# Short-convolution layer on one core: product e of the input projection also by seven smaller products in ten chunks, with 26 instead of 32 pages

## The chip, the core and the metric

The kernel runs on one core of a Trainium2 chip. The metric is the device time of one execution in microseconds. Before the change its median over 3 runs is 773.18 us (772.85 to 773.5). The engines are named as in the profile: PE is TensorE's matmul, PEld its weight load, DVE is VectorE, ACT is ScalarE, POOL is GpSimd, and SP is SyncE, which issues most of the DMAs.

## The reference

One layer (`DEPTH = 1`), so only the short-convolution mixer is computed. `x` is 1 x 1024 x 1024 in float32.

```python
u = rms_norm(x, pre_norm)
z, bg, cg, v = jnp.split(u @ w_in, 4, axis=-1)          # w_in: 1024 x 8192
y = bg * causal_dwconv(cg * v, conv_w) * jax.nn.silu(z)  # conv of width 3 along the sequence
m = y @ w_out                                            # w_out: 2048 x 1024
out = x + rms_norm(m, post_norm)
```

## The kernel before, in words

**The input projection.** The 2048 inner channels are cut into 16 chunks `c` of 128. Each chunk has two pairs of channel blocks, `p = 2c` for (`cg`, `v`) and `p = 2c + 1` for (`z`, `bg`). For one pair the product of a 2 x 2 block matrix of weights with the 2 x 2 block matrix of activations is computed by Winograd's form of Strassen's rule: seven products `a` to `g` in place of eight. Each is 128 channels by 512 positions with 512 rows to sum over, so four slices `k`. In float32 accuracy a product of one slice is three matmuls in the format fp32r: low part of the weights by high part of the activations, high by low, high by high. A product of one pair is therefore 12 matmuls with 512 columns. Names: `u_a` to `u_g` are the activations of a product; `wah`, `wal` to `wgh`, `wgl` the high and low parts of its weights; `raw` the loaded weight blocks; `se`, `sc`, `sf`, and `raw` overwritten for `d`, the sums of weight blocks that the rule asks for, made on POOL or DVE; `px`, `pv`, `py` the PSUM banks that collect the products; `sna`, `snc`, `sne` copies of a bank in SBUF to which later banks are added.

**Seven smaller products.** For `b`, `f` and `g` the rule is applied a second time in most chunks (`by_seven`): the 2 x 2 blocks are then the two pairs of a chunk by two halves of 256 rows, and the positions are halved too. Each of the seven sub-products `a'` to `g'`, for the two pairs together, is six matmuls with 256 columns. Their weight sums are `dsb`, `dsf`, `dsg`, their split weights `dwb`, `dwf`, `dwg`, their activations `ub..._deep` and so on, their PSUM banks `px2b`, `py2b`, `pv2b` and so on. Products `a`, `c`, `d` and `e` are done whole, pair by pair.

**Splitting.** A weight `t` is split by an ACT copy that rounds to fp32r (`wah`) and a DVE subtraction `t - wah`. In `split` that subtraction reads both operands from SBUF. In `split_by_bank` ACT also copies `t` into a PSUM bank, `beside`, and the subtraction reads one operand from there. Before the change there is one such bank, held for the whole of the projection and reused by every copy.

**After the projection.** The convolution is one ACT multiplication and two DVE steps over 1024 positions per chunk (`cv<-gpad,cw,cv`), in chunk `c + 1`'s time. The output projection (`po_`, `pb_`, `pf_` banks) is another pass by the same rule.

**What sets the order.** All instructions are first recorded; then `Plan.arrange` puts each engine's instructions in an order, by due times that go back from PE's order and by costs that the planner assumes, with a table `boost` that moves the due time of single instructions. PE's own order is written out by the list `slots`, a list of products and sub-products. Each engine then runs its list strictly in order, and waits at an instruction until its operands and its buffer are there. SBUF buffers of 2 KB per partition, the pages, hold all weights, sums and copies; there are `PAGES` of them, and a load on SP waits in its queue until its page is free. PSUM has eight banks in one pool. All instructions are issued in one helper, so nearly all have the line L252 in the profile before.

Of the kernel before, what the change touches and what calls it, by code (L numbers as in the profile page):

```python
# [18 lines left out]
PAGES = 32  # L19
DEEP = 2  # L20
DEEP_F = 2
DEEP_G = 2
LEAD = 7.0
HEAD_SLOTS = (
    0, 23, 31, 30, 29, 28, 27, 26, 25, 24, 22, 21, 20, 1, 19, 18, 2, 17, 16, 15, 14, 3, 13, 12, 11, 10, 4, 7, 9, 8,
    5, 6, 31, 29, 30, 28, 23, 0, 10, 11, 27, 26, 7, 4, 29, 15, 31, 16, 13, 3, 21, 22, 1, 20, 26, 27, 25, 30, 4, 7,
)
PLAN = {
    "end": 14.0,
    "psum": 3.0,  # L30
    "store": 6.0,
    "turns": 1,
    "apart": 11.0,
    "hard": 2.0,
    "lock": 0.3,
    "sum": 10.0,
# [578 lines left out]
def kernel(  # L615
# [70 lines left out]
    ug_d = dram.tile([P, KH, HB], F32, tag="ug_d", name="ug_d")  # L686
    uf_d = dram.tile([P, CQ // 2, HB // 2], F32, tag="uf_d", name="uf_d")
# [1378 lines left out]
```

## Time and profile before

| what | before |
|---|---|
| median of 3 runs | 773.18 us |
| profiled execution | 772.83 us |
| its span | 771.0 us, granted clock 0.998 |
| PE busy | 762.2 us (99%), 4320 matmuls |
| DVE busy | 673.9 us (87%), 1022 instructions |
| ACT busy | 458.8 us (60%), 880 instructions |
| POOL busy | 462.2 us (60%), 416 instructions |
| DMA | 130.11 MB, mean 169 GB/s |

The profiled execution is 1.8 us longer than its span; what lies around the span is taken as unchanged. Busy time is the union of an engine's instructions. A matmul's duration in the trace is longer than the distance to the next matmul, since matmuls overlap in the array; what counts for the time is the distance from start to start.

### The profile page before, as it was taken

The numbers are of one execution on the slowest core, as the hardware profiler recorded it, in microseconds if no ns is written. First come the engines' busy times: TensorE is split into PE (matmuls) and PEld (weight loads), VectorE is DVE, ScalarE is ACT, GpSimd is POOL, SyncE is SP. The second block draws the span as 40 slices with busy tenths as digits, with TensorE's granted clock in tenths as the row PEclk, the third lists the DMA queues.
The fourth block names the chain that finished last, engine by engine and source line by source line (L and its number), as shares of the span: only waits on it lengthen the run. The fifth ranks groups of instructions, "written<-read, shape, count | busy, mean of one in ns | idle before, by whom it ended". The sixth has DMA issues, their size and how long they took to land.

```text
span 771.0 us, 12816 instructions
## 1 busy us (share of the span) xinstructions
PE 762.2 (99%) x4320; PEld 669.6 (87%) x4320; DVE 673.9 (87%) x1022; ACT 458.8 (60%) x880; POOL 462.2 (60%) x416
## 2 busy tenths in 40 slices
PE   8999999999999999999999999999999999999996
PEld 7888889898889898888888898988888889889885
DVE  6899988989988978989999989798999898877993
ACT  7765678575656565556556565556653656564831
POOL 2519997889575778696789777584739100600321
PEclk9999999999999999999999999999999999999999
DMA  9222325243333547576858474927465998666842
GB/s 318 66 56 82 119 85 152 101 126 131 97 116 96 171 111 209 126 191 158 239 137 254 116 215 107 249 84 213 122 180 174 335 367 293 197 218 206 274 150 109
DMA packets 117137, 130.11 MB, mean 169 GB/s; under 512 B 7320, under 2 KB 74704, under 8 KB 116944
## 3 DMA queue, kind: packets, MB, share of 16 engines
q1 hardware_dynamic: 112560, 120.77, 49.0%
q0 software_dynamic: 4352, 8.39, 7.1%
q8 instruction: 34, 0.56, 0.3%
q14 instruction: 31, 0.25, 0.1%
q10 hardware_dynamic: 160, 0.14, 0.0%
HBM read 101.74 MB, written 44.30 MB: 189 GB/s over the span
## 4 chain that ended last, share of the span: by engine, by line
PE 98%; DVE 1%; DMA 0%; ACT 0%; POOL 0%; issue 0%; POOLq 0%; ACTq 0%
PE px L252 39%; PE pv L252 15%; PE po_x L252 11%; PE px2b L252 5%; PE px2f L252 4%; PE px2g L252 3%; PE po_v L252 3%; PE pp L252 3%; PE pv2b L252 3%; PE pv2f L252 2%; PE pf_x L252 1%; PE pb_x L252 1%; PE py2b L252 1%; PE pv2g L252 1%; PE py L252 1%; PE pf_v L252 1%
## 5 line engine op out<-in xcount | busy, mean ns | idle before, releaser
L252 PE MATMUL px<-u_d,wdh 128*128 128x512 f32 x248 | 76.8, 390 | 0.0
L252 PE MATMUL px<-u_a,wah 128*128 128x512 f32 x248 | 76.7, 390 | 0.0
L252 PE MATMUL pv<-u_e,weh 128*128 128x512 f32 x248 | 76.7, 390 | 0.0
L252 PE MATMUL px<-u_c,wch 128*128 128x512 f32 x248 | 76.6, 390 | 0.0
L252 ACT COPY beside<-raw 128x512 f32<-128x512 f32 x67 | 39.6, 591 | 31.8 <-DVE wal L252 11.0
L252 PEld LDWEIGHTS px<-u_d,wdh 128*128 128x128 f32 x248 | 46.6, 188 | 9.1
L252 PEld LDWEIGHTS px<-u_c,wch 128*128 128x128 f32 x248 | 46.7, 188 | 9.0
L252 PEld LDWEIGHTS px<-u_a,wah 128*128 128x128 f32 x248 | 46.7, 188 | 8.9
L252 PEld LDWEIGHTS pv<-u_e,weh 128*128 128x128 f32 x248 | 46.6, 188 | 8.9
L252 DVE SCALAR_TENSOR_TENSOR cv<-gpad,cw,cv 128x1024 f32<-128x1024 f32 x32 | 49.7, 1554 | 3.4 <-ACT cv L252 3.3
L252 POOL TENSOR_TENSOR sf<-raw,sc 128x512 f32<-128x512 f32 x30 | 44.5, 1482 | 10.9 <-DVE sc L252 6.0
L252 PE MATMUL px<-u_d,wdl 128*128 128x512 f32 x124 | 48.7, 393 | 0.0
L252 PE MATMUL px<-u_a,wal 128*128 128x512 f32 x124 | 48.7, 393 | 0.0
L252 PE MATMUL px<-u_c,wcl 128*128 128x512 f32 x124 | 48.5, 392 | 0.0
L252 PE MATMUL pv<-u_e,wel 128*128 128x512 f32 x124 | 48.5, 391 | 0.0
L252 POOL TENSOR_TENSOR sc<-se,raw 128x512 f32<-128x512 f32 x25 | 36.5, 1460 | 19.0 <-DVE se L252 10.0
L252 ACT COPY sna<-px 128x512 f32<-128x512 f32 x30 | 17.6, 586 | 49.4 <-PE px L252 47.7
L252 POOL TENSOR_TENSOR raw<-raw,raw 128x512 f32<-128x512 f32 x31 | 44.8, 1446 | 3.3 <-DVE se L252 1.9
L252 POOL TENSOR_TENSOR rs_post<-ve_post,minus_half 128x1 f32<-128x1 f32 x7 | 5.4, 784 | 68.1 <-DVE ve_post L252 68.1
L252 POOL TENSOR_TENSOR se<-raw,raw 128x512 f32<-128x512 f32 x22 | 33.1, 1504 | 17.7 <-DMA raw<-in_sc_w_in 5.7
L252 DVE TENSOR_TENSOR wcl<-sc,wch 128x512 fp32r<-128x512 f32 x31 | 31.6, 1020 | 2.6 <-ACT wch L252 2.6
L252 DVE TENSOR_TENSOR sna<-px2b,sna 128x256 f32<-128x256 f32 x56 | 23.2, 413 | 11.9 <-PE px2b L252 11.9
(486 smaller groups left out, 2637.1 us busy)
## 6 DMA issues: line engine op xcount, KB each, us to landing
raw<-in_sc_w_in SPq DMA_DIRECT2D x128, 256.0 KB, 4.6
y_d<-cv SPq DMA_DIRECT2D x16, 512.0 KB, 3.1
s_d<-s SPq DMA_DIRECT2D x32, 256.0 KB, 4.8
t_d<-in_sc_w_out POOLq DMA_DIRECT2D x16, 512.0 KB, 8.2
tb<-in_sc_w_out SPq DMA_DIRECT2D x16, 256.0 KB, 3.0
t_d<-in_sc_w_out SPq DMA_DIRECT2D x16, 256.0 KB, 4.5
t_d<-t_d SPq DMA_DIRECT2D x16, 256.0 KB, 4.5
s<-y_d SPq DMA_DIRECT2D x16, 256.0 KB, 4.7
```

Source lines behind the costliest of these rows:

```text
L252: getattr(engine, name)(*(self.plain(a) for a in args), **{k: self.plain(a) for k, a in kw.items()})
```

## The change

1. `by_seven` takes in `e`: in chunks 4 to 13, ten of them, product `e` of both pairs is computed by seven sub-products of 256 columns. Their accumulators are `px2e`, `pv2e` and the two `pv` banks; `deep_after_e` puts them together through the pages `es0`, `es1`. Weight sums are `dse`, split weights `dwe`, activations `ue..._deep`, made once under chunk 3 from a copy of `u_e` kept in DRAM (`ue_d`).
2. In these chunks PE does `e` first: its sub-products stand under `c`, `d` and `a` of the chunk's first pair, those of `b` begin only behind them, and all of `f` and `g` follow in the second pair. The copy `sne` of the first pair now starts from `d`'s bank, and `e` is added later.
3. `PAGES` goes from 32 to 26, and the pool of split activations from 18 to 24 buffers. In the ten chunks the lower weight rows for `g` are loaded a second time (`fetch_far`, tiles `rg`), so that the first copy's pages are given back before; the early weight splits of the head move to a pool of their own.
4. `beside` takes any free PSUM bank for each copy and gives it back. Also `wc`, `dwf1`, `dwg0` to `dwg2` and the new `dwe0` to `dwe2` are split through a bank.
5. The planner's numbers and the `boost` table are new.

```diff
-PAGES = 32
+PAGES = 26
+DEEP_E = 4
...
-        0: -1.88, 1: 31.37, 2: -1.93, 4: 16.59, 5: 18.27, 6: 0.14, 20: 0.84, 21: 1.2, 22: 10.67, 27: -0.09,
+        7: -0.46, 56: -1.96, 59: 1.16, 101: 0.11, 164: -0.46, 165: -3.22, 184: -0.96, 201: -0.26, 206: -0.48,
...
-BY_BANK_DEEP = (("b", 0), ("b", 1), ("b", 2), ("f", 0), ("f", 2))
+BY_BANK_DEEP = (("f", 1), ("g", 0), ("g", 1), ("g", 2), ("e", 0), ("e", 1), ("e", 2), ("b", 0), ("b", 1), ("b", 2), ("f", 0), ("f", 2))
...
-    LAST = {"b": NC, "f": NC - 1, "g": NC - 2}
+    LAST = {"b": NC, "f": NC - 1, "g": NC - 2, "e": NC - 2}
...
     def beside():
-        if not beside_bank:
-            beside_bank.append(bank("beside"))
-        return beside_bank[0]
+        beside_bank.append(bank(f"beside_{len(beside_bank)}"))
+        return beside_bank[-1]
...
-            if i in "adg" and by_seven("f", p // 2):
+            if i in "acdg" and by_seven("f", p // 2):
...
+        elif i == "d" and p % 2 == 0 and by_seven("e", c):
+            t = sn[p, "e"] = page(f"sne_{p}")
+            nc.scalar.copy(t, x_)
...
+    def fetch_far(c):
+
+        for p in (2 * c, 2 * c + 1):
+            far[p] = flat(page(f"rg_{p}", shape=(KH, P)))
+            c0 = PAIRS[p][1][1] * CI + c * P
+            nc.sync.dma_start(far[p].rearrange("p (a b) -> p a b", a=KH), wiv[:, KH:, c0 : c0 + P])
...
+    def deep_after_e(c, i):
+
+        if i == "b'":
+            return
+        p = 2 * c
+        x_, e_ = (banks.get((c, "e" + k)) for k in ("x'", "v'"))
+        if i == "a'":
+            deep["e", c, 0] = page(f"es0_{c}")
+        elif i == "d'":
+            deep["e", c, 1] = page(f"es1_{c}", shape=(HH,))
+        t = deep["e", c, int(i in ("d'", "g'"))]
+        if i in ("a'", "c'", "d'"):
+            nc.scalar.copy(t[:, HH:] if i == "c'" else t[:, :HH], x_[:, :HH])
+        elif i == "f'":
+            v_ = banks[p, "v"]
+            nc.vector.tensor_add(t[:, HH:], e_[:, :HH], t[:, HH:])
+            nc.vector.tensor_add(v_, v_, t)
+            nc.vector.tensor_add(sn[p, "e"], v_, sn[p, "e"])
+        elif i == "g'":
+            v_ = banks[p + 1, "v"]
+            nc.vector.tensor_add(v_[:, HH:], e_[:, :HH], t)
+            nc.vector.tensor_add(v_[:, :HH], v_[:, :HH], t)
+            sn[p + 1, "e"] = t = page(f"sne_{p + 1}")
+            nc.scalar.copy(t, v_)
...
+    EVEN_E = {"c": "ea eb ee ec", "d": "ef ed eg", "a": "ba bb be bc"}
+    ODD_E = {"c": "bf bd fa fe bg fb", "d": "fc ff fg fd ga gb gf", "a": "gc ge gg gd"}
...
-        for i in "ced" if f7 else "cedf":
+        for i in "cd" if e7 else "ced" if f7 else "cedf":
...
+        ("d", 2 * DEEP_E - 2): lambda: load_u("e"),
+        ("c", 2 * DEEP_E - 1): lambda: deep_subs("e", [0, 1]),
+        ("e", 2 * DEEP_E - 1): lambda: [deep_split("e", i, True) for i in ("e'", "c'")],
+        ("d", 2 * DEEP_E - 1): lambda: [deep_split("e", i, True) for i in ("d'", "g'")],
```

How the order moves is shown in chunk 9. First PE before, at product `e` of pair 18, the first of that chunk; `pv` is its bank, `wel` and `weh` its weights.

```order
L252 MATMUL pv_18_4176<-u_e_88,wel_18_4082 128x512
L252 MATMUL pv_18_4176<-u_e_88,weh_18_4031 128x512 x2
L252 MATMUL pv_18_4176<-u_e_88,wel_18_4082 128x512
L252 MATMUL pv_18_4176<-u_e_88,weh_18_4031 128x512 x2
L252 MATMUL pv_18_4176<-u_e_88,wel_18_4082 128x512
L252 MATMUL pv_18_4176<-u_e_88,weh_18_4031 128x512 x2
L252 MATMUL pv_18_4176<-u_e_88,wel_18_4082 128x512
L252 MATMUL pv_18_4176<-u_e_88,weh_18_4031 128x512 x2
```

These twelve wide matmuls stand once for pair 18 and once more, a half chunk later, for pair 19. In the same place the changed kernel has the first three sub-products, which serve both pairs.

```order
L337 MATMUL px2e_9_4638<-u_e_89,dwe0l_9_4580 128x256
L337 MATMUL px2e_9_4638<-u_e_89,dwe0h_9_4561 128x256 x2
L337 MATMUL px2e_9_4638<-u_e_89,dwe0l_9_4580 128x256
L337 MATMUL px2e_9_4638<-u_e_89,dwe0h_9_4561 128x256 x2
L337 MATMUL pv_18_4650<-u_e_89,dwe0l_9_4580 128x256
L337 MATMUL pv_18_4650<-u_e_89,dwe0h_9_4561 128x256 x2
L337 MATMUL pv_18_4650<-u_e_89,dwe0l_9_4580 128x256
L337 MATMUL pv_18_4650<-u_e_89,dwe0h_9_4561 128x256 x2
L337 MATMUL pv2e_9_4659<-u_e_89,dwe1l_9_4623 128x256
L337 MATMUL pv2e_9_4659<-u_e_89,dwe1h_9_4613 128x256 x2
L337 MATMUL pv2e_9_4659<-u_e_89,dwe1l_9_4623 128x256
L337 MATMUL pv2e_9_4659<-u_e_89,dwe1h_9_4613 128x256 x2
```

Twenty-four wide matmuls of a chunk have become forty-two narrow ones, and three banks (`px2e`, `pv`, `pv2e`) are opened one after another while the banks of the chunk before are still being read. Next DVE before, at the same place: the convolution steps of chunk 8 (`cv_8`), the adds that end chunk 8's `g` (`gs1`, `px_17`), and the first adds of chunk 9's `b` (`sna_18`).

```order
L252 SCALAR_TENSOR_TENSOR cv_8_4167<-gpad_643,cw_77,cv_8_4167 128x1024
L252 TENSOR_TENSOR gs1_8_4192<-pv2g_8_4121,gs1_8_4192 128x256
L252 SCALAR_TENSOR_TENSOR cv_8_4167<-gpad_643,cw_77,cv_8_4167 128x1024
L252 TENSOR_TENSOR px_17_3819<-px_17_3819,gs1_8_4192 128x512
L252 TENSOR_TENSOR sna_18_4102<-px2b_9_4202,sna_18_4102 128x256
L252 TENSOR_TENSOR cv_8_4167<-px_17_3819,cv_8_4167 128x512
L252 TENSOR_TENSOR sna_18_4102<-py2b_9_4211,sna_18_4102 128x256
L252 TENSOR_TENSOR dwb1l_9_4239<-beside_861,dwb1h_9_4181 128x512
```

And DVE in the changed kernel, from the adds of `g` on.

```order
L337 TENSOR_TENSOR gs1_8_4618<-pv2g_8_4574,gs1_8_4618 128x256
L337 TENSOR_TENSOR px_17_4237<-px_17_4237,gs1_8_4618 128x512
L337 SCALAR_TENSOR_TENSOR cv_8_4626<-gpad_648,cw_77,cv_8_4626 128x1024 x2
L337 TENSOR_TENSOR dwe3_9_4656<-se_19_4568,dwe3_9_4656 128x256
L337 TENSOR_TENSOR dwe2l_9_4688<-beside_139_4641,dwe2h_9_4675 128x512
L337 TENSOR_TENSOR wal_19_4694<-beside_140_4634,wah_19_4685 128x512
L337 TENSOR_TENSOR es0_9_4661<-pv2e_9_4659,es0_9_4661 128x256
L337 TENSOR_TENSOR cv_8_4626<-px_17_4237,cv_8_4626 128x512
L337 TENSOR_TENSOR dwb0l_9_4711<-beside_141_4701,dwb0h_9_4669 128x512
L337 TENSOR_TENSOR cv_8_4626<-cv_8_4626,sna_17_4269 128x512
L337 TENSOR_TENSOR pv_18_4650<-pv_18_4650,es0_9_4661 128x512
```

Both convolution steps now stand together behind the adds of `g`, with the splits of `e`'s weights right behind them, and the multiplication that gives bank `px_17` back stands five instructions behind the steps. The copies have a bank of their own each (`beside_139` to `beside_141`), where they had one in common (`beside_861`).

More of the change, by code (lines that the diff above doesn't have):

```diff
@@ L22 @@
 DEEP_G = 2
+DEEP_E = 4
 LEAD = 7.0
 HEAD_SLOTS = (
-    0, 23, 31, 30, 29, 28, 27, 26, 25, 24, 22, 21, 20, 1, 19, 18, 2, 17, 16, 15, 14, 3, 13, 12, 11, 10, 4, 7, 9, 8,
-    5, 6, 31, 29, 30, 28, 23, 0, 10, 11, 27, 26, 7, 4, 29, 15, 31, 16, 13, 3, 21, 22, 1, 20, 26, 27, 25, 30, 4, 7,
+    0, 17, 25, 24, 23, 22, 21, 20, 19, 18, 16, 15, 14, 13, 12, 1, 2, 3, 4, 9, 11, 10, 5, 6, 8, 7, 25, 23, 24, 22,
+    17, 0, 3, 2, 21, 20, 9, 4, 7, 8, 2, 3, 19, 25, 20, 21, 4, 9, 18, 8, 7, 25,
 )
 PLAN = {
-    "end": 14.0,
-    "psum": 3.0,
-    "store": 6.0,
+    "end": 14.18,
+    "psum": 0.61,
+    "store": 6.47,
     "turns": 1,
     "apart": 11.0,
-    "hard": 2.0,
-    "lock": 0.3,
-    "sum": 10.0,
+    "hard": 2.74,
+    "lock": 0.28,
+    "sum": 11.74,
     "early": 0.0,
@@ L1052, in high_plain @@
         for k in ks:
-            plain_w[p, n, k] = [page(f"wn{n}{k}{h}_{p}", F32R) for h in "hl"]
+            plain_w[p, n, k] = [hp.tile([P, HB], F32R, tag="wn", name=f"wn{n}{k}{h}_{p}", bufs=12) for h in "hl"]
             nc.scalar.copy(plain_w[p, n, k][0], block(p, n, k))
@@ L1409, in deep_product @@
             ps, first = banks[2 * c + (i == "g'"), "v"], False
+        elif z == "e" and i in ("b'", "f'", "g'"):
+            p = 2 * c + (i == "g'")
+            first = i != "f'"
+            if first:
+                banks[p, "v"] = bank(f"pv_{p}")
+            ps = banks[p, "v"][:, HH if i == "f'" else 0 :]
         elif z == "g" and i in ("b'", "f'", "g'"):
@@ L1434, in deep_after @@
             if late_conv(c):
-                split_high(2 * c + 2, "c")
+                if not by_seven("e", c):
+                    split_high(2 * c + 2, "c")
             elif c == NC - 1:
@@ L1463, in deep_after_f @@
             nc.vector.tensor_add(both, ps.unsqueeze(1).broadcast_to([P, 2, HH]), both)
-            split_low(2 * c + 2, "c")
+            if not by_seven("e", c):
+                split_low(2 * c + 2, "c")
             if not late_conv(c):
@@ L1471, in deep_after_f @@
             nc.vector.tensor_mul(g[:, HH:], t, sn[p, "e"][:, HH:])
+    def deep_after_e(c, i):
[21 more added lines that the diff above has]
+            nc.scalar.copy(t, v_)
     def deep_after_g(c, i):
-        if i == "g'" and late_conv(c):
+        if i == "g'" and late_conv(c) and not by_seven("e", c):
             conv_tap(c, 1)
@@ L1498, in deep_after_g @@
                 gate(c)
-                for part in (0, 1):
+                for part in (0, 1) if not by_seven("e", c + 1) else ():
                     deep_sums("b", c + 1, part)
@@ L1622 @@
         q, c = p + 1, p // 2
-        f7, g7 = (by_seven(z, c) for z in "fg")
+        f7, g7, e7 = (by_seven(z, c) for z in "fge")
         if p % 2 == 0:
-            sub = {"e": "ba bb", "a": "bc be", "d": "fa fb"}
+            sub = EVEN_E if e7 else {"e": "ba bb", "a": "bc be", "d": "fa fb"}
             if not f7:
                 sub |= {"d": "", "f": "gb ga", "a": "bc be gf"}
+        elif e7:
+            sub = ODD_E
         elif f7:
@@ L1762 @@
                 deep_sums("b", p // 2, 1)
-        elif i == "e":
-            add_s(q, "ecdf" if f7 else "ec")
+        e7 = by_seven("e", p // 2)
+        if i == ("c" if e7 else "e"):
+            add_s(q, "cdf" if e7 and p % 2 == 0 else "ecdf" if f7 else "ec")
+            if e7 and p % 2:
+                fetch_far(p // 2)
+            if e7 and p % 2 == 0:
+                for part in (0, 1):
+                    deep_sums("b", p // 2, part)
             if f7 and p % 2 == 0:
@@ L1779 @@
             out_sums(p)
-        elif i == "d":
+        if i == ("c" if by_seven("e", prev) and e7 else "d" if e7 else "e") and p % 2 == 0 and p > 2 and late_conv(prev):
+            fetch_s(prev)
+            conv_tap(prev, 2)
+            nc.gpsimd.tensor_mul(cvs[prev][:, HB:], cvs[prev][:, HB:], sn[p - 1, "e"])
+            last_muls(prev)
+            done[prev] = cvs.pop(prev)
+        if i == "d":
             if p + 2 <= END:
                 fetch(p + 2)
+            if p % 2 and by_seven("e", q // 2):
+                add_s(p + 2, "e")
+                for part in (0, 1):
+                    deep_sums("e", q // 2, part)
             if not f7:
```

40 lines of the change are left out of this document (21 added, 19 removed), and 158 rows, old and new, of the table PLAN.

## The prediction, made before the result was known

> **What bounds the kernel now.** I read the page first, then the list of waits for PE, then the busy time by chunk, and last the timelines of PE and DVE inside one chunk. From the page and from the waits of PE:
>
> ```profile
> span 771.0 us, 12816 instructions
> PE 762.2 (99%) x4320; PEld 669.6 (87%) x4320; DVE 673.9 (87%) x1022; ACT 458.8 (60%) x880; POOL 462.2 (60%) x416
> PE pw L252 <- DVE idle L252: 1.1, 1, 1.1
> PE pp L252 <- ACT u_a L252: 0.5, 1, 0.5
> PE pk L252 <- DVE xa L252: 0.3, 1, 0.3
> ```
>
> PE is busy for all but 8.8 us, and its three waits, 1.9 us together, lie in the start-up. So before the change there is nothing to gain but matmul time, and everything to lose by a wait of PE. The stretches by chunk (columns: stretch, its length, then busy PE, PEld, DVE, ACT, POOL, clock, DMA share, GB/s) are chunks 2 and 3, and chunks 4 to 13 as one row, the ten that change:
>
> ```profile
> 105.70:142.62 36.92, 36.92 (x224) 32.98 (x223) 32.50 (x55) 31.64 (x73) 29.63 (x30) 1.00 0.37 108
> 142.62:179.54 36.92, 36.92 (x224) 32.98 (x223) 34.39 (x50) 23.17 (x46) 32.03 (x29) 1.00 0.35 111
> 179.54:548.74 369.20, 369.20 (x2222) 329.81 (x2221) 327.70 (x506) 214.44 (x410) 270.43 (x247) 1.00 0.59 160
> ```
>
> Every chunk takes 36.92 us and PE is busy for all of it, at full clock. In the ten chunks DVE has 32.77 us of work per chunk, ACT 21.44, POOL 27.04. DVE is second, with 4.15 us to spare.
>
> **What a sub-product costs on PE.** One product `e` and what follows it, in the timeline of PE (start, duration, instruction):
>
> ```profile
> 414.30 0.40 PE L252 MATMUL pv<-u_e,wel 128*128 128x512 f32 x1
> ...
> 417.04 0.28 PE L252 MATMUL pv2b<-u_b,dwb2l 128*128 128x256 f32 x1
> ...
> 417.76 0.28 PE L252 MATMUL pv2f<-u_f,dwf2l 128*128 128x256 f32 x1
> ...
> 418.48 0.28 PE L252 MATMUL px2b<-ubdh_deep,dwb2l 128*128 128x256 f32 x1
> ...
> 419.19 0.28 PE L252 MATMUL px2f<-ufdh_deep,dwf2l 128*128 128x256 f32 x1
> ...
> 419.89 0.40 PE L252 MATMUL px<-u_d,wdl 128*128 128x512 f32 x1
> ```
>
> From start to start the twelve wide matmuls of `e` take 2.74 us (228 ns each), and a sub-product of six narrow ones 0.72, 0.72, 0.71, 0.70 us (119 ns each). A narrow matmul is thus a little dearer than half a wide one, and the rule's saving of one eighth shrinks. Per chunk the change removes 2 x 2.74 = 5.48 us and adds 7 x 0.713 = 4.99 us: 0.49 us saved, 4.9 us in ten chunks. Bounds: all sub-products at 0.72 give 4.4, all at 0.70 give 5.8.
>
> The Trainium skill speaks against the change here. "TensorE: Matmul & The Clock Gate", section Back-to-back issue gap, gives a sustained spacing of 81 ns for 128 columns and 131 ns for 512; a straight line between would put 256 columns at 98 ns (an estimate from that page), and 42 x 98 against 24 x 131 ns would cost 0.97 us per chunk instead of saving 0.49. The rows above do not agree with it, for these fp32r matmuls at least, and they decide.
>
> **What it costs the other engines.** The groups of instructions that the change removes or repeats (count, then busy time, mean ns of one), DVE first; the last two lines are DVE's timeline:
>
> ```profile
> L252 DVE TENSOR_TENSOR wel<-se,weh 128x512 fp32r<-128x512 f32 x31 | 30.7, 989 | 0.7 <-PE pv2b L252 0.7
> L252 DVE TENSOR_TENSOR wcl<-sc,wch 128x512 fp32r<-128x512 f32 x31 | 31.6, 1020 | 2.6 <-ACT wch L252 2.6
> L252 DVE TENSOR_TENSOR wdl<-beside,wdh 128x512 fp32r<-128x512 f32 x26 | 17.8, 684 | 5.3 <-ACT beside L252 4.3 <-POOL dsg L252 0.7 <-issue 0.4
> L252 DVE TENSOR_TENSOR dwf1l<-dsf,dwf1h 128x512 fp32r<-128x512 f32 x13 | 11.7, 897 | 2.4 <-ACT dwf1h L252 2.2
> L252 DVE TENSOR_TENSOR dwg2l<-dsg,dwg2h 128x512 fp32r<-128x512 f32 x12 | 10.4, 867 | 0.3 <-ACT dwg2h L252 0.3
> L252 DVE TENSOR_TENSOR dwg<-raw,dwg 128x256 fp32r<-128x256 f32 x12 | 10.9, 910 | 0.0
> L252 DVE TENSOR_TENSOR gs<-pv2g,gs 128x256 f32<-128x256 f32 x24 | 10.0, 415 | 1.9 <-PE pv2g L252 1.9
> L252 DVE TENSOR_TENSOR px<-px,gs 128x512 f32<-128x512 f32 x24 | 16.6, 690 | 0.3
> 290.34 0.68 DVE L252 TENSOR_TENSOR px<-px,gs 128x512 f32<-128x512 f32 x1
> 290.94 0.41 DVE L252 TENSOR_TENSOR sna<-px2b,sna 128x256 f32<-128x256 f32 x1
> ```
>
> Two instructions in a row overlap by 0.08 us (0.68 long, 0.60 to the next start), so each counts as its mean less 0.08. DVE per chunk: two `wel` go, -1.82. Three `dwe` splits through a bank come, priced as `wdl`, +1.81, and a fourth of half size from SBUF, priced as `dwg`, +0.83. Two `wcl`, one `dwf1l`, `dwg1l` and `dwg2l` each now read a bank: -2 x 0.34 - 0.21 - 2 x 0.18 = -1.25. Putting `e` together takes three adds of 256 (as `gs`) and one of 512 (as `px`): 3 x 0.33 + 0.61 = +1.61. By the new order DVE holds some 14 more of the sums that POOL or DVE can make, at 0.3 to 0.9 us each, +0.1 per chunk if they are even and +0.4 where they gather; I take +0.4, as the chunks are not even. The sum is +1.6, with bounds +0.8 (the half-size split at 0.33, no moved sums) and +2.3 (moved sums and splits at the dearest mean). DVE then has 34.3 us of work in a chunk of 36.43: 94%, with 2.1 us to spare for everything it waits for in order.
>
> ```profile
> L252 ACT COPY beside<-raw 128x512 f32<-128x512 f32 x67 | 39.6, 591 | 31.8 <-DVE wal L252 11.0 <-DVE dwf2l L252 10.9 <-DVE dwf0l L252 5.9
> L252 ACT CAST weh<-se 128x512 fp32r<-128x512 f32 x31 | 19.2, 620 | 4.1 <-DVE se L252 1.5 <-PE py2b L252 1.4 <-POOL se L252 1.2
> L252 ACT COPY gs<-px2g 128x256 f32<-128x256 f32 x36 | 13.4, 372 | 11.7 <-PE px2g L252 11.6
> L252 POOL TENSOR_TENSOR dsf<-sf,sf 128x256 f32<-128x256 f32 x13 | 14.3, 1098 | 0.0
> L252 POOL TENSOR_TENSOR raw<-raw,raw 128x512 f32<-128x512 f32 x31 | 44.8, 1446 | 3.3 <-DVE se L252 1.9 <-PE px2g L252 1.0
> ```
>
> ACT per chunk gets about ten more `beside` copies (6.1 us), one cast more and one of half size (1.0) and three copies as `gs` (1.1): 29.7 us, 81%. POOL gets 3.3 sums for `dse` (3.6) and loses 0.7 `raw` (1.0) among smaller exchanges: near 30 us, 82%.
>
> That such loads can be carried is seen in the rows by chunk. In chunk 3 DVE worked 34.39 and POOL 32.03 of 36.92 us at once, in chunk 2 ACT 31.64, and PE waited in neither. But nowhere are all three so full, and nowhere ten chunks in a row. How thin the cover is at times:
>
> ```profile
> 419.01 0.68 DVE L252 TENSOR_TENSOR wdl<-beside,wdh 128x512 fp32r<-128x512 f32 x1
> ```
>
> This split ends at 419.69, and PE's matmul from it starts at 419.89 (above), with 0.20 us to spare.
>
> **One-time work.** Under chunk 3 come four activation splits for `e` through banks, 4 x 0.60 = 2.4 us on DVE, less 1.25 from the other splits there: 34.39 becomes 35.5 of 36.92. Chunk 2 has 4.4 us idle, into which part can go. Restoring `u_e` behind the tenth chunk is one or two splits, hidden.
>
> **The sum.** Matmuls -4.9 us. New waits of PE: none before; with DVE's spare time halved I take 1.5 us over the whole span. Bounds are 0 (chunk 3's load, no wait) and 4.5 (chunk 3 left DVE 2.53 us idle; if it cannot do with less, a chunk takes 34.35 + 2.53 = 36.88, 0.45 more than its matmuls). I lean to the lower end, since chunk 3's PE had no wait to show at all. Start-up and the end behind the last matmul stay. The profiled execution goes from 772.83 to 769.4. The median of the runs stands 0.35 above it: **769.8 us**.
>
> **Rivals.**
>
> *DVE needs the idle time it has had.* The upper bound just worked out: of 4.9 us saved 4.5 go in waits, 772.8, no change. For it speaks that DVE runs strictly in order; against it, that the instructions it waits on are other engines', reordered too. Chance 0.14.
>
> *PSUM banks run out and PE waits, slower than before.* Place: the start of a chunk. There `px2e`, `pv` and `pv2e` are opened while both `px` banks of the last chunk, its `pv2g`, the new `px` and at least one `beside` are held: eight of eight. `px` of the last chunk's second pair comes free by a multiplication that stands behind two convolution steps:
>
> ```profile
> L252 DVE SCALAR_TENSOR_TENSOR cv<-gpad,cw,cv 128x1024 f32<-128x1024 f32 x32 | 49.7, 1554 | 3.4 <-ACT cv L252 3.3
> ```
>
> If PE has to wait for half a step in each chunk, 10 x 0.78 = 7.8 us come in and the result is 773.2 - 4.9 + 7.8 = 776.1; for a whole step it is 783.8. It decides from 0.64 us per chunk on. For it: banks were fewer in use before, with `beside` fixed at one. Against: `b` and `f`, which opened banks there, now come later. Chance 0.14.
>
> *Pages run out.* With 32 pages the loads already wait for pages in SP's queue, and a load takes 4.6 us to land:
>
> ```profile
> SPq L252 <- PE px L252: 48.8, 27, 10.0
> raw<-in_sc_w_in SPq DMA_DIRECT2D x128, 256.0 KB, 4.6
> ```
>
> With 26 pages and 20 more loads, two weights that come a whole landing late cost 9.2 us: 777.5. Chance 0.05; I count it as slower.
>
> *Narrow matmuls of `e` cost more than 131 ns* (5.48 us over 42), so that the change doesn't save what it says. Then PE's time alone grows: at 140 ns by 0.4 us per chunk, 777.2. The same shapes for `b` and `f` show 119 ns in this trace; chance 0.01.
>
> **How the numbers follow.** My forecast has 0.66. About 0.2% (1.5 us) is what a measurement of this kernel can tell from no change, so faster means below 771.6 and slower above 774.7. Same gets the second rival's 0.14 and 0.01 of the others' mild forms, slower 0.19. The range goes from 767.8 (no wait, 5.4 us saved) to 776.0 (the bank rival at its mild end) and leaves out the worse forms.
>
> **What would show it.** Right: chunks 4 to 13 at 36.4 to 36.6 us, the `e` sub-products at 0.70 to 0.72 us, DVE near 34 us per chunk, PE's waits in the middle under 3 us together. Wrong: PE waits for DVE's `dwe`, `dwg` or `es` groups in many chunks, a bank wait at `pv2e`, waits on `raw` loads; or a chunk below 36.3 us, which would mean that the narrow matmuls are cheaper than taken.

## The result, and the profile after

| kernel | median | runs from to | ratio to before |
|---|---|---|---|
| before | 773.29 us | 772.85 to 773.75 | |
| after | 780.38 us | 774.22 to 783.5 | 1.0082 [1.0059, 1.0104] |

The forecast was 769.8 us. After is slower by 0.8%, and it scatters by 9 us where before scatters by 0.9. Its profiled execution, 774.91 us, is one of its shortest. The same kernel was profiled once more (`again`, 781.06 us); most readings below are from that trace. From the page of after and of `again`, and from the waits of PE in `again`:

```profile
PE 760.0 (98%) x4500; PEld 674.1 (87%) x4500; DVE 678.1 (88%) x1108; ACT 532.0 (69%) x1050; POOL 462.6 (60%) x443
```
```profile
PE 763.6 (98%) x4500; PEld 676.6 (87%) x4500; DVE 675.1 (87%) x1108; ACT 532.0 (68%) x1050; POOL 463.2 (59%) x443
PE px L337 <- DVE dwg2l L337: 3.9, 1, 3.9
PE px L337 <- DVE wal L337: 1.5, 2, 0.8
PE px L337 <- DVE wcl L337: 0.6, 1, 0.6
```

DVE has hardly more to do than before (673.9), and PE waits in few places, but long. The stretches of `again`, each from the first sub-product of `e` of a chunk to the next (columns as in the prediction), are chunks 5 to 10:

```profile
215.17:251.66 36.49, 36.49 (x241) 33.50 (x240) 33.04 (x58) 28.38 (x58) 30.82 (x31) 1.00 0.41 126
251.66:288.16 36.50, 36.50 (x242) 33.50 (x240) 32.48 (x57) 27.44 (x56) 28.78 (x29) 1.00 0.50 157
288.16:324.65 36.49, 36.49 (x242) 33.50 (x240) 33.19 (x59) 27.24 (x54) 27.04 (x28) 1.00 0.68 185
324.65:363.45 38.80, 37.27 (x242) 33.68 (x240) 33.40 (x60) 28.02 (x56) 27.12 (x28) 1.00 0.72 188
363.45:406.48 43.03, 39.00 (x242) 34.76 (x241) 32.97 (x57) 27.18 (x55) 29.93 (x31) 0.96 0.60 175
406.48:444.04 37.56, 36.92 (x242) 33.53 (x241) 34.83 (x59) 27.79 (x55) 29.22 (x30) 1.00 0.73 204
```

An undisturbed chunk takes 36.49 us in place of 36.92, with 33 us of DVE, 27 to 28 of ACT, 27 to 31 of POOL and no wait of PE. Chunks 8 and 9 take 2.3 and 6.5 us more, chunk 10 takes 1.1 more. The chain behind the longest wait, in chunk 9, first on PE, then on POOL:

```profile
391.45 0.40 PE L337 MATMUL px<-u_g,dwg0h 128*128 128x256 f32 x2
395.74 0.39 PE L337 MATMUL px<-u_g,dwg2l 128*128 128x256 f32 x1 [3.89 <-DVE dwg2l L337]
397.08 1.05 PE L337 MATMUL px<-u_a,wah 128*128 128x512 f32 x2
397.94 0.63 PE L337 MATMUL px<-u_a,wal 128*128 128x512 f32 x1
```
```profile
380.02 1.18 POOL L337 DMA_DIRECT2D t_d<-in_sc_w_out  x1
384.33 0.74 POOL L337 TENSOR_TENSOR dsg<-dsg,rg 128x256 f32<-128x256 f32 x1 [3.12 <-DMA rg<-in_sc_w_in]
389.64 1.29 POOL L337 TENSOR_TENSOR se<-raw,raw 128x512 f32<-128x512 f32 x1 [4.58 <-DVE snc L337]
390.89 0.92 POOL L337 TENSOR_TENSOR gpad<-snc,sne 128x256 f32<-128x256 f32 x1
391.78 1.26 POOL L337 TENSOR_TENSOR raw<-raw,raw 128x512 f32<-128x512 f32 x1
393.00 0.72 POOL L337 TENSOR_TENSOR dsg<-rg,dsg 128x256 f32<-128x256 f32 x1
```

POOL waits 3.12 us for the second load of `g`'s weights (`rg`), then 4.58 us before `se`. That wait is put down to DVE, but the second of its two `raw` loads landed at 389.5 in the trace, and `se` starts right behind it, so it is the load. The last `dsg`, from which `dwg2l` is split, stands behind `se` in POOL's list and inherits both waits. The kernel before had the same wait for late loads in chunk 9, but had made all four `dsg` ahead of it, from weights that lay in the pages already:

```profile
376.32 1.19 POOL L252 TENSOR_TENSOR dsg<-raw 128x256 f32<-128x256 f32 x1
378.98 0.92 POOL L252 TENSOR_TENSOR dsg<-raw,dsg 128x256 f32<-128x256 f32 x1
384.84 1.32 POOL L252 TENSOR_TENSOR se<-raw,raw 128x512 f32<-128x512 f32 x1 [4.94 <-DMA raw<-in_sc_w_in]
```

Why the loads are late shows in SP's and POOL's issues in chunk 8, and in the DMA view of the same stretch (count, size, median us to landing). First before, then `again`:

```profile
336.21 2.24 SPq L252 DMA_DIRECT2D raw<-in_sc_w_in  x4
342.22 1.18 POOL L252 DMA_DIRECT2D t_d<-in_sc_w_out  x1
raw<-in_sc_w_in SPq DMA_DIRECT2D x5, 256.0 KB, 5.5
```
```profile
337.42 1.00 SPq L337 DMA_DIRECT2D rg<-in_sc_w_in  x2
338.44 1.18 POOL L337 DMA_DIRECT2D t_d<-in_sc_w_out  x1
338.47 3.40 SPq L337 DMA_DIRECT2D raw<-in_sc_w_in  x4
raw<-in_sc_w_in SPq DMA_DIRECT2D x4, 256.0 KB, 8.4
```

Before, the four loads were issued 4 us ahead of POOL's accumulating DMA (`t_d`, 512 KB) and landed in 5.5 us. Now two `rg` loads go ahead of them on SP, the accumulating DMA is issued at the same moment, and they take 8.4. All 16 DMA engines are then full, and POOL works 2.97 us of the first 5 and 0.54 of the next (stretches of 5 us; shares above 1 are as the view gives them):

```profile
340.00:345.00 5.00, 5.00 (x41) 4.84 (x40) 4.04 (x9) 1.58 (x3) 2.97 (x4) 1.00 1.04 199
345.00:350.00 5.00, 4.69 (x28) 3.99 (x28) 2.60 (x6) 3.65 (x8) 0.54 (x1) 1.00 1.09 341
```

In chunk 8 the late load reaches PE by way of ACT, and it is the first of the four that counts. ACT waits for it before it makes `wah`, and the splits of `f` behind that come late to DVE, and so to PE:

```profile
346.35 0.62 ACT L337 CAST wah<-raw 128x512 fp32r<-128x512 f32 x1 [2.27 <-DMA raw<-in_sc_w_in]
347.31 0.43 DVE L337 TENSOR_TENSOR dwf<-sf,dwf 128x256 fp32r<-128x256 f32 x1 [2.33 <-ACT dwf L337]
```

### The profile page after: what moved, and what is told of

It is laid out like the page before. It is cut to its first block, busy times and chain, and to the rows that moved or that the text cites. A ratio compares the mean times of both kernels' runs of the same rounds, so it can differ in the third digit from the quotient of the medians.

```text
span 773.1 us, 13660 instructions
## 1 busy us (share of the span) xinstructions
PE 760.0 (98%) x4500; PEld 674.1 (87%) x4500; DVE 678.1 (88%) x1108; ACT 532.0 (69%) x1050; POOL 462.6 (60%) x443
## 4 chain that ended last, share of the span: by engine, by line
PE 91%; DVE 3%; ACT 2%; DMA 2%; issue 1%; POOL 1%; SPq 0%; DVEq 0%; POOLq 0%; ACTq 0%
PE px L337 37%; PE po_x L337 11%; PE pv L337 10%; PE px2b L337 5%; PE px2f L337 3%; PE px2g L337 3%; PE po_v L337 3%; PE pp L337 3%; PE pv2b L337 3%; PE px2e L337 2%; PE pv2f L337 2%; PE pf_x L337 1%; PE pb_x L337 1%; DMA raw<-in_sc_w_in 1%; PE py2b L337 1%
## 5 line engine op out<-in xcount | busy, mean ns | idle before, releaser
L337 POOL TENSOR_TENSOR sc<-se,raw 128x512 f32<-128x512 f32 x30 | 46.0, 1532 | 5.8 <-DMA raw<-in_sc_w_in 2.7
L337 DVE SCALAR_TENSOR_TENSOR cv<-gpad,cw,cv 128x1024 f32<-128x1024 f32 x32 | 46.7, 1459 | 1.1 <-ACT cv L337 1.1
L337 POOL TENSOR_TENSOR sf<-raw,sc 128x512 f32<-128x512 f32 x31 | 42.2, 1363 | 3.9 <-issue 2.5
L337 POOL TENSOR_TENSOR se<-raw,raw 128x512 f32<-128x512 f32 x23 | 31.3, 1363 | 20.9 <-DMA raw<-in_sc_w_in 8.1
L337 POOL TENSOR_TENSOR ry_f<-ry_f 128x256 f32<-128x256 f32 x2 | 11.2, 5598 | 45.2 <-DMA ry_f<-s_d 45.2
L337 POOL TENSOR_TENSOR raw<-raw,raw 128x512 f32<-128x512 f32 x24 | 33.9, 1413 | 2.9 <-DVE se L337 2.4
L337 POOL TENSOR_TENSOR cv<-cv,sne 128x512 f32<-128x512 f32 x13 | 18.0, 1385 | 18.7 <-DVE cv L337 18.7
L337 PEld LDWEIGHTS px<-u_a,wal 128*128 128x128 f32 x124 | 23.3, 188 | 5.6 <-DVE wal L337 0.8
L337 PEld LDWEIGHTS px<-u_c,wcl 128*128 128x128 f32 x124 | 23.3, 188 | 5.0 <-ACT sna L337 1.0
L337 ACT COPY snc<-px 128x512 f32<-128x512 f32 x31 | 18.1, 584 | 13.7 <-PE px L337 13.1
```

The lines of the kernel that those rows point to most:

```text
L337: getattr(engine, name)(*(self.plain(a) for a in args), **{k: self.plain(a) for k, a in kw.items()})
```

## The experiments

The kernel before, timed beside each of these, had medians of 773.1 to 773.5 us. Each keeps the order of after instruction by instruction, but for the edit told. The table gives the profiled executions by stretch, from the starts of `py2b` in PE's timeline; 7.78 us, by which `b` stands later in its chunk when `e` goes first, are taken off the first column and put onto the fifth. A wait at the head of chunk 10 counts in chunk 9 here.

| kernel | to chunk 5 | 5 to 7 | 8 | 9 | 10 to 13 | rest | median of the runs |
|---|---|---|---|---|---|---|---|
| before | 216.47 | 110.76 | 36.92 | 36.92 | 147.68 | 222.28 | 773.29 |
| after | 219.32 | 109.47 | 37.27 | 39.04 | 146.00 | 222.02 | 780.38 |
| again | 218.62 | 109.47 | 38.80 | 44.02 | 146.32 | 222.03 | 781.09 |
| pages32 | 216.39 | 109.47 | 38.59 | 43.04 | 148.10 | 222.04 | 779.67 |
| pages26_fu | 218.52 | 109.47 | 39.13 | 43.72 | 146.15 | 222.03 | 781.61 |
| no_acc | 218.83 | 109.47 | 36.95 | 39.25 | 146.04 | 221.97 | 773.93 |
| no_rg | 218.63 | 109.47 | 36.54 | 38.08 | 146.16 | 222.21 | 773.63 |
| rg_unused | 218.57 | 109.47 | 39.67 | 43.95 | 148.36 | 222.13 | 782.52 |
| acc_late | 218.93 | 109.47 | 36.95 | 38.67 | 149.21 | 222.03 | 777.09 |
| sums_late | 218.25 | 109.47 | 36.91 | 40.17 | 148.00 | 222.03 | 776.63 |
| sums_early | 218.76 | 113.83 | 40.19 | 38.69 | 147.31 | 222.03 | 783.23 |
| both | 219.21 | 109.47 | 38.01 | 39.99 | 146.17 | 222.04 | 776.82 |
| pool_sums | 218.91 | 109.47 | 37.07 | 40.61 | 146.30 | 222.03 | 776.70 |
| pad_later | 219.01 | 109.47 | 37.07 | 38.86 | 146.04 | 222.03 | 774.72 |

### First round: DVE, pages or queue

`again` is after, unchanged.

> The changed kernel once more, unchanged. It shows where the time of a typical execution goes, since the first profile caught one of the shortest (774.9 us of 774.2 to 783.5). All theories: median 778 to 782 with a spread of several us, while the kernel before stays within 1 us. Theory DVE (DVE, with 94% of a chunk filled in a fixed order, hands PE its weights late): PE's waits sit on DVE splits in many chunks. Theory LOADS (weight loads land too late, since with 26 pages and a second load of g's rows SP issues them late): the waits sit in the chunks in which POOL and ACT first wait for raw and rg loads. Theory BANKS (PSUM runs out): PE waits at the first matmul of px2e, pv2e or another new bank.

Measured 781.09 us, 1.0094 [1.007, 1.0118]. The loss is there again, in the same two chunks and larger.

`taps_half` takes work off DVE:

```diff
-nc.vector.scalar_tensor_tensor(cv, src, w, cv2)
+nc.vector.scalar_tensor_tensor(cv[:, :512], src[:, :512], w, cv2[:, :512])
```

> The changed kernel with its order of instructions kept, but the two convolution steps on DVE done over 512 instead of 1024 positions in each chunk (half of the convolution's later taps is left out). That takes about 2 x 0.55 us per chunk from DVE and nothing else. Theory DVE: the waits go, median 768 to 770, spread under 2 us. Theory LOADS: DVE only passes the delay on; median above 776, the spread stays. Theory BANKS: px of the last chunk comes free 1.1 us earlier, so also a good part of the loss gone, 770 to 774, and PE's waits at new banks vanish.

Measured 778.04 us, 1.0048 [1.0035, 1.0061]. Chunk 8 took 40.48 us, chunk 9 39.19: they still lose 6.7 us together. The edit took less off DVE than was meant. A halved step takes 0.74 us in place of 1.27 where it runs freely, but many took 1.2 to 1.9, and DVE's busy time fell only from 675.1 to 670.8 us. So this run says little about DVE's load by itself. What speaks against it is that PE never waits in chunks 5 to 7, with as much DVE work, and that `no_rg` below has none of the waits in chunks 8 and 9 with DVE busy for 677.9 us.

`pages32` gives the loads, weights and sums 32 pages again; for room in SBUF, `e`'s sub-products `c'`, `d'`, `g'` take `f`'s activations, and their own splits are left out.

> The changed kernel with its order kept, but with 32 pages handed out in the same sequence; the room comes from leaving out e's own split activations c', d', g' (the sub-products of e read those of f; twelve copies and three subtractions under chunk 3 go with them). Loads whose page is the hold-up are issued up to six pages earlier. Theory LOADS by pages: median 768 to 771. Theory LOADS by SP's order (loads stand in SP's queue behind stores that wait for DVE): no change, 778 to 782. Theory DVE and BANKS: 777 to 782, only chunk 3 is relieved.

Measured 779.67 us, 1.0084 [1.0065, 1.0104]. 2.2 us of the way to chunk 5 are won, chunks 8 and 9 stay near what they were.

`stores_free` lets SP's stores of `y_d` and `s_d` take their data from `u_a`, so that SP does not wait for DVE.

> The changed kernel with its order kept, but the stores of y and of its sums to DRAM take their data from a tile that is always there (the stored values are left out of the computation, the bytes moved are the same). So SP never waits for DVE at these stores, and the loads behind them in its queue go out earlier. Theory LOADS by SP's order: median 768 to 771. Theory LOADS by pages: little change, above 776. Theory DVE and BANKS: above 777.

Measured 776.94 us, 1.0047 [1.0035, 1.0059]. About half of the loss went by the median, and the runs scatter by 1.7 us. In its trace chunks 8 and 9 took 37.71 and 39.01 us, close to the short execution of after (37.27 and 39.04). So SP's waits at its stores have a share in the loss. The theory of SP's order had forecast 768 to 771 us and holds in part at most.

### Second round: the collision on the DMA engines

`no_acc` drops all sixteen accumulating DMAs.

```diff
-nc.gpsimd.dma_start(to, src, accum_op=ALU.add)
```

> The changed kernel with its order kept, but all sixteen accumulating DMAs on POOL (the sums of output weights, t_d) left out, so the output product works from unsummed weights. COLLISION (weight loads that are issued just before they are needed share the DMA engines with POOL's accumulating DMA and land 8 to 9 us late, in chunks 8 and 9): chunks 8 and 9 go from 37-44 us to about 36.5, the about 3 us around chunks 2 to 4 stay, total 771 to 773, and the repetitions lie within 2 us of each other. LOADS by too few pages: the loads are late for want of a page, not of DMA time; chunks 8 and 9 stay over 38 us, total 777 or more. DVE full: the same, 777 or more.

Measured 773.93 us, 1.0011 [1.0002, 1.0019], from 773.46 to 775.61: most of the loss and of the scatter is gone. Chunk 9 keeps 2.8 us of it, as in the short execution of after. In chunk 8 the raw loads are issued in the same place as in `again`, behind two `rg` loads, and land in 5.7 us in place of 8.4.

`pages26_fu` has the leaving-out of `pages32` with 26 pages.

> Order kept and 26 pages, but e's sub-products c', d' and g' take f's activations, and the splits of e's own activations (four through banks under chunk 3, among others) are left out, as in pages32 before, which had 32 pages besides. It tells what of pages32's gain in chunks 2 to 4 (3 us) came from where. If the one-time splits cost it: up to chunk 4 as in pages32, about 2.5 to 3 us less than after. If the pages did: no change against after there. Chunks 8 and 9 are not touched by it: total 776 to 782.

Measured 781.61 us, 1.0099 [1.0075, 1.0123]. The way to chunk 5 stays at 218.5: it was the pages that won 2.1 us there, and not the splits. That is the price of giving up six pages, and it has nothing to do with chunks 8 and 9.

`acc_late` and `sums_late` leave nothing out and move the sums to where the DMA engines are idle.

```diff
 POOL, chunk 8 (chunk 9 likewise)
-DMA t_d (accumulating)
 dsg0, dsg0, dsg1, dsg1, se_18, raw_18, sc_18, sf_18, DMA t_d, dse0, dse0, raw_19, dse1, dse1
+DMA t_d (accumulating)
```

> Nothing left out. In POOL's list only two of the sixteen accumulating DMAs move: the one in chunk 8 (at 338 us) goes some 23 us later, behind the dse sums, and the one in chunk 9 (at 380 us) some 30 us later, behind a convolution sum, both to where the DMA engines have little to do. COLLISION: raw loads of chunks 8 and 9 land in 5 us in place of 8 to 9, most of the loss there goes, total 772 to 775. If the four copies on SP beside them are as much to blame, half of it: 776 to 778. DVE or pages: no change, 778 to 782.

> As acc_late, and four of SP's copies t_d<-t_d (two from each of chunks 8 and 9) go behind the next load of s, into the same quiet stretch. COLLISION: chunks 8 and 9 at 36.5 to 36.8 us, the about 3 us around chunks 2 to 4 stay, total 771.5 to 773. DVE or pages: 778 to 782.

Measured 777.09 us, 1.005 [1.0038, 1.0062], and 776.63 us, 1.0042 [1.003, 1.0054]. Half of the loss went. Chunk 8 is at 36.9 in both, but new waits come up in chunk 10, into which the moved transfers now reach.

### Third round: the second loads of g

`sums_early` moves the sums the other way, ahead of the loads; `soon` fetches `rg` of pair 18 earlier and makes the last `dsg` ahead of `se`; `early_soon` does both.

```diff
 SP, chunk 9
 DMA rg_19
+DMA rg_18
 DMA tx_d, tb_d, s_d, raw_20, s_d
-DMA rg_18
```

> Nothing left out; only DMAs of t_d move in the order. The accumulating DMA of chunk 8 goes 10 us earlier (338 to about 328 us) and that of chunk 9 12 us earlier (380 to about 368), and SP's copies beside the weight loads of chunks 8 and 9 go to three stretches in which the DMA engines had little to do (about 323, 358 and 403 us). no_acc left 773.9 and about 3 us of losses in chunks 8 and 9 that copies and the second loads of g's weights could make. COLLISION: the weight loads of chunks 8 and 9 land in 3 to 5 us, chunks 8, 9 and 10 at 36.5 to 37.2 us, total 772 to 774. If it is only g's second load (rg) that comes late: chunk 9 stays at 38 to 39, total 775 to 777.

> Nothing left out and no DMA of t_d moved. In chunk 9 the second load of g's weights for pair 18 (rg) is issued right behind that for pair 19, about 5 us earlier than before (the two pages that it and a raw load use are exchanged from there on), and POOL makes the second dsg sum ahead of se. SECOND LOAD (what PE waits for in chunk 9 is dwg2l, made from rg, which is fetched just before it is needed, since its page comes free late): the wait at dwg2l, 0.5 to 3.9 us, goes, and with it the slower matmuls behind it; chunk 9 at 37.5 to 38.5, chunk 8 as it was, total 775 to 777. COLLISION alone: the load is late wherever it is issued, 778 to 782.

> Both edits, of sums_early and of soon; nothing left out. If the two causes add up: chunks 8, 9 and 10 at 36.5 to 36.8 us; what stays is the about 2 to 3 us around chunks 2 to 4: total 771 to 772.5, faster than before by a little. If collision alone decides: as sums_early.

Measured 783.23 us, 1.013 [1.0115, 1.0146]; 777.82 us, 1.0053 [1.0041, 1.0066]; 784.48 us, 1.0142 [1.0128, 1.0156]. The raw loads of chunk 8 landed in 5.8 to 6.1 us in `sums_early`, and yet it is the slowest but one. The reason is on DVE and POOL, in the timelines at the new wait (4.20 us, in front of `py2b`):

```profile
331.68 0.68 DVE L337 TENSOR_TENSOR pv<-pv,es 128x512 f32<-128x512 f32 x1
332.28 6.78 DVE L337 TENSOR_TENSOR cv<-cv,sna 128x512 f32<-128x512 f32 x1
338.98 0.42 DVE L337 TENSOR_TENSOR pv<-pv,es 128x256 f32<-128x256 f32 x1
```
```profile
330.75 1.73 POOL L337 TENSOR_TENSOR cv<-cv,sne 128x512 f32<-128x512 f32 x1
332.71 1.71 POOL L337 TENSOR_TENSOR sf<-raw,sc 128x512 f32<-128x512 f32 x1
333.97 1.14 POOL L337 TENSOR_TENSOR t<-tb,tb 128x256 f32<-128x256 f32 x1
338.57 1.07 POOL L337 TENSOR_TENSOR dsf<-dsf,sf 128x256 f32<-128x256 f32 x1
```

A DVE sum with both operands in SBUF takes 6.78 us, ten times its usual 0.68, while POOL works through ten instructions without a pause. Sums with an operand in PSUM, as the first line's, keep their time. The Trainium skill has the rule behind it ("SBUF — State Buffer", section Who interferes with whom): a DVE instruction with two SBUF inputs and a GpSimd instruction that reads SBUF share a port, and one waits for the other. The trace agrees, and shows that the wait can outlast one instruction. The port itself is not seen in a trace: what the runs show is which sums are long, and beside what.

`no_rg` leaves the twenty second loads out; what is made from them reads part of `u_a`.

> The changed kernel with its order kept, but without the twenty second loads of g's weights (rg): the sums and copies made from them read part of u_a in their place, so g's products come out of wrong weights. The pages stay 26. SECOND LOAD: no engine waits for rg any more; the wait at dwg2l goes, chunk 9 at 37 to 38, total 774 to 776. COLLISION through the raw loads alone: the raw loads still land in 8 to 9 us beside the accumulating DMAs, se is late and so is all behind it, chunks 8 and 9 over 38: 777 to 781.

Measured 773.63 us, 1.0 [0.9991, 1.0009]. Leaving out `rg` does as much as leaving out the accumulating DMAs. Either of the two removes most of the loss, so it takes both to make it. In chunk 8 the first raw load is now issued at 338.00 us, 0.45 us ahead of POOL's accumulating DMA, and lands in 2.9 us; ACT no longer waits for it:

```profile
343.80 0.62 ACT L337 CAST wah<-raw 128x512 fp32r<-128x512 f32 x1
```

The third and fourth, issued behind that DMA, still take 7.6 and 7.7 us, and `se` is made only 1 us earlier than in `again`, and yet the chunk takes 36.54 us. So not every late load costs time there, only the one for which ACT waits.

### Fourth round: bytes or waiting, and a repair

`rg_unused` issues the loads, but nobody reads them.

```diff
-nc.gpsimd.tensor_sub(dsg0, dsg0, rg_18)   # and the other readers of rg
+nc.gpsimd.tensor_sub(dsg0, dsg0, u_a[...])
```

> The changed kernel with its order kept and all twenty second loads of g's weights (rg) issued as before, but the sums and copies made from them read part of u_a, as in no_rg (g's products come out of wrong weights), so nobody waits for rg. JUST IN TIME (the loss comes from engines that run strictly in order and wait for a load issued too shortly before): as no_rg, chunks 8 and 9 at 36.5 and 38.1, total 773 to 775. BYTES (rg's 5 MB delay the raw loads beside it): as after, chunks 8 and 9 over 38, total 778 to 781.

Measured 782.52 us, 1.0109 [1.0094, 1.0124]. My theory of this round, that engines wait for `rg` because it is fetched too late, falls as the whole cause: with nobody waiting for it the loss is all there. POOL then waits 7.84 us in one piece for the raw loads of `se` in chunk 9, where `again` has 3.12 for `rg` and 4.58 for them. It is `rg` ahead of the raw loads that makes these late. Whether by its bytes, or by the half microsecond by which it moves them behind POOL's DMA, is not separated. The DMA view of chunk 9 in `no_rg`, and then in `rg_unused`:

```profile
raw<-in_sc_w_in SPq DMA_DIRECT2D x4, 256.0 KB, 4.0
t_d<-in_sc_w_out POOLq DMA_DIRECT2D x1, 512.0 KB, 9.7
```
```profile
raw<-in_sc_w_in SPq DMA_DIRECT2D x3, 256.0 KB, 7.7
t_d<-in_sc_w_out POOLq DMA_DIRECT2D x1, 512.0 KB, 9.4
```

`rg_soon` moves that one load only; `after_loads` puts the accumulating DMAs of chunks 8 and 9 behind the `se` that waits for the loads, and SP's copies of `t_d` behind the loads; `both` does both.

> As soon, without the change on POOL: only one DMA moves, the second load of g's weights for pair 18 in chunk 9, to some 4 to 5 us earlier. JUST IN TIME: the wait at dwg2l in chunk 9 goes, and nothing takes its place there; chunk 9 at 37 to 38, chunk 8 as after; total 775 to 777.5, at most as soon (777.8). BYTES: 779 to 781.

> Nothing left out. In chunks 8 and 9 the accumulating DMAs move on POOL only to behind the se sum that waits for the raw loads (some 6 to 8 us later), the third one some 6 us later, and SP's copies of t_d to behind those chunks' raw loads. Neither POOL nor DVE gets an instruction earlier than before, as they did in sums_early. COLLISION: raw_18 and raw_20 land in 3 to 5 us; chunks 8 and 9 at 36.5 to 37.5, total 773 to 776. If the loss moves to chunk 10, as in acc_late: 776 to 778.

> after_loads and rg_soon together; nothing left out. If the two causes add up: chunks 8 to 10 at 36.5 to 37 us, and only the about 2 us of the start-up stay: total 771 to 773.5, level with the kernel before or a little faster. If either alone has got what there is: as the better of the two.

Measured 778.12 us, 1.0061 [1.0038, 1.0084]; 778.68 us, 1.006 [1.0048, 1.0072]; 776.82 us, 1.0039 [1.0027, 1.0051]. In the trace of `rg_soon` the wait at `dwg2l` is gone and chunk 9 takes 38.45 us, while chunk 8 keeps its loss (38.77). Its raw loads in chunk 9 land in 3.3 to 4.3 us, so when `rg` is issued matters as well; but its runs go from 775.61 to 781.63. In `after_loads` the raw loads land in 4.9 to 5.3 us (8.4 and 7.7 in `again`), and PE waits all the same, for another reason. In `both`, chunk 9:

```profile
387.40 0.42 DVE L337 TENSOR_TENSOR snc<-px2f,snc 128x256 f32<-128x256 f32 x1
387.74 2.70 DVE L337 TENSOR_TENSOR dsg<-rg,rg 128x256 f32<-128x256 f32 x1
```

Here it is the same blocked kind of sum, beside POOL's unbroken work from 383.8 to 391.6. `pool_sums` moves that sum and the one of chunk 8 to POOL; `pad_later` also puts DVE's next sum behind the splits for which PE waits:

```diff
 DVE, chunk 9
-gpad<-snc,sne
 dwg2l<-beside,dwg2h
 wal<-beside,wah
 snc<-px2f,snc
 wcl<-beside,wch
+gpad<-snc,sne
```

> As both, and two sums with two operands in SBUF go from DVE to POOL: gpad in chunk 8, half of the second dsg in chunk 9, which POOL now makes right behind se. In both the loads landed in 3 to 6 us, yet DVE's dsg sum took 2.70 us in place of 0.42 and its gpad sum 1.91 beside POOL instructions that followed each other without a pause, and PE waited 1.3 us behind each. BLOCKED SUMS (that is what is left of the loss there): both waits go, chunks 8 and 9 at 36.5 to 37.3, total 773 to 774.5. If another wait lies right behind: as both, 776 to 777.

> As pool_sums, and DVE makes its gpad sum of chunk 9 four instructions later, behind dwg2l, wal and wcl, which have an operand in PSUM. In pool_sums the gain in chunk 8 (38.0 to 37.1 us) was lost in chunk 9: now gpad was the sum that took 2.92 us in place of 0.42 beside POOL's unbroken work, ahead of dwg2l, for which PE waited 2.1 us. BLOCKED SUMS: the wait at dwg2l shrinks from 2.1 to under 0.7 us, chunk 9 at 37.5 to 38.5, total 774 to 775.5; what is left over the kernel before is the start-up. If not: 776 to 777.5.

Measured 776.7 us, 1.0043 [1.0029, 1.0057], and 774.72 us, 1.0015 [1.0006, 1.0024], from 774.3 to 775.77. In `pool_sums` the block only moved on to the next sum, in `pad_later` it is gone:

```profile
388.39 2.92 DVE L337 TENSOR_TENSOR gpad<-snc,sne 128x256 f32<-128x256 f32 x1
391.24 0.68 DVE L337 TENSOR_TENSOR dwg2l<-beside,dwg2h 128x512 fp32r<-128x512 f32 x1
```
```profile
388.49 0.68 DVE L337 TENSOR_TENSOR dwg2l<-beside,dwg2h 128x512 fp32r<-128x512 f32 x1
393.23 0.42 DVE L337 TENSOR_TENSOR gpad<-snc,sne 128x256 f32<-128x256 f32 x1
```

`pad_later` computes everything and moves about a dozen instructions. It wins back 5.7 of the 7.1 us. No version that computes everything beat the kernel before: the way to chunk 5 still takes 3.0 us more than it should (216.47 less the 0.43 saved in chunk 4), chunks 8 and 9 together another 3.0, and the 4.3 us of the matmuls with 0.3 at the end do not cover that.

## Why the prediction was wrong

- **The matmuls: right, but for a little.** Chunks were to take 36.43 us; all undisturbed ones take 36.49 or 36.50. Of 4.9 us 4.3 came, just under the lower bound of 4.4.
- **The load of the engines: not the trouble, and put somewhat too high.** DVE was put at 34.3 us per chunk and shows 32.5 to 34.8 in the rows above, ACT at 29.7 and shows 27.2 to 28.4, POOL near 30 and shows 27.0 to 30.8. Over chunks 4 to 12 DVE's mean is 33.3 us in `again` and 33.7 in after, 0.7 and 1.1 above the same chunks of before, where 1.6 was forecast. The rival that DVE needs the idle time it has had does not explain the loss: in chunks 5 to 7 PE never waits, and `no_rg` has the same load on DVE without the waits in chunks 8 and 9.
- **New waits of PE, 1.5 us with bounds 0 and 4.5: this is the step that failed.** It was worked out from DVE's spare time alone, and the lower end was chosen since chunk 3 of before, so loaded, had no wait; but chunk 3 has a DMA share of 0.35. The trace of `again` loses 2.3 us in chunk 8, 7.5 in chunk 9 and 0.4 behind, 10.2 in place of 1.5, and 2.6 more up to chunk 5: 12.8 us against 4.3 + 0.3 gained, which is the 8.2 us by which its span is longer. What the runs show in the place of that step is waits for loads: PE waits for splits whose weights come late, since `rg` loads and POOL's accumulating DMA are on the DMA engines with them, and without either most of it is gone. In the sum the twenty `rg` loads got no price on the DMA engines at all, nor did the place of POOL's accumulating DMAs among SP's issues, which in the new order is 6 us nearer to the loads in chunk 8. Among the signs of being wrong, "waits on `raw` loads" is the one that came.
- **What I read wrongly in the profile of before.** The ten chunks were read as one row, with a DMA share of 0.59. By chunk it goes from 0.35 to 0.72; chunks 5, 8, 9 and 10 of before:

```profile
216.46:253.38 36.92, 36.92 (x224) 32.98 (x223) 30.01 (x50) 21.53 (x43) 24.91 (x25) 1.00 0.35 111
...
327.22:364.14 36.92, 36.92 (x224) 32.98 (x223) 32.42 (x52) 22.27 (x44) 28.07 (x27) 1.00 0.71 182
364.14:401.06 36.92, 36.92 (x224) 32.98 (x223) 33.84 (x49) 20.80 (x40) 30.27 (x28) 1.00 0.72 197
401.06:437.98 36.92, 36.92 (x224) 32.98 (x223) 33.98 (x53) 21.49 (x43) 29.23 (x26) 1.00 0.66 175
```

The two fullest chunks of before are the two that broke. The share alone does not tell, though: chunk 7 of `again` has 0.68 and loses nothing. The trace of before also had late loads there already (`se` waited 4.94 us); nothing behind them was urgent then.
- **Start-up taken as unchanged, and the one-time work under chunk 3 as hidden: wrong by 2.6 us together.** In `again` 1.1 us of it lie ahead of chunk 2 and 1.5 in chunks 2 to 4. 2.1 of the 2.6 come from the pages (`pages32` against `pages26_fu`), to which the sum gave no price.
- **"Pages run out", 777.5 us:** the right neighbourhood, late raw loads, and nearly the right size, but the wrong cause for chunks 8 and 9, which 32 pages didn't help. Its 0.05 was too little. That its 777.5 lies near the result is luck as far as chunks 8 and 9 go. The bank rival did not show: none of the waits of PE in `again` is for a bank at the head of a chunk.
- **Two slips that change nothing:** the lower bound of DVE's rise adds up to 0.7, not 0.8, and the 0.14 that "same" gets is that of the rival listed first.

Chunk 9 differs by 5 us between the two traces of the same kernel, and the 5 us add up: PE waits 0.46 us for `dwg2l` in after and 3.89 in `again`, and the slower matmuls behind the long wait add 1.6. The raw loads issued at 378 to 380 us took 5.0 to 5.4 us in after, 6.4 to 9.1 in `again`. In after both went out ahead of POOL's accumulating DMA, by 0.9 and 0.4 us; in `again` the second, for which `se` waits, went out 0.4 us behind it. What stays open is why the issues shift from one execution to the next, and no run moves this order by so little.

## What to carry over

A load's price is its place among the other queues' transfers: look at the DMA share by stage as well as over the span, and at what an extra load pushes back in its own queue and past which large DMA. Where a strictly ordered engine waits for a load, ask what stands behind the waiting instruction; the same wait cost nothing before and 4 us of PE after. An engine that catches up without a pause is not harmless either: in these runs DVE's sums from SBUF were held up beside POOL's unbroken work. And look in the trace how much an edit really took off an engine before reading a time as a verdict: `taps_half` halved the work of DVE's convolution steps and took 4.3 of 675.1 us off DVE.

## What the runs showed of the hardware

- 256 KB loads issued with a 512 KB accumulating DMA of POOL's or behind it, beside SP's copies, took 7.7 to 9.2 us to land (medians; `again`, `rg_unused`). In the same place they took 5.7 us without that DMA (`no_acc`, chunk 8) and 5.3 with it moved behind them (`after_loads`). Being just ahead was not always enough: in chunk 9 of before three loads issued 0.3 to 1.7 us ahead of it took 6.6 to 9.3.
- A DVE sum of two SBUF operands took 2.70 and 2.92 us in place of 0.42, and 6.78 in place of 0.68, beside POOL instructions without a gap.
- After the wait of 3.89 us the wide matmuls ran at 0.43 us each (two in 397.08 to 397.94) in place of 0.23, for about 3 us, so the wait cost about 1.6 us more than its length. The stretch shows a granted clock of 0.96. Waits of 3.37 us (`pages32`), 3.66 (`pages26_fu`) and 4.31 (`rg_unused`) had such a stretch behind them too, waits of 2.36 (`after_loads`) and 2.09 (`pool_sums`) had none. The Trainium skill ("TensorE: Matmul & The Clock Gate", section What's actually happening) has TensorE fall to half rate after an idle window of about 3.4 us; the waits of these runs agree, 3.37 us being about that long.
